# The state space layer's scaled C matrices: their transfers issued by GpSimd in place of ScalarE

## The chip, the cores and the metric

The kernel runs on one core of a Trainium2 chip. The metric is the time of one execution on the device in microseconds (us), as the median of several runs. The work is fp32 throughout; large matrix products are made as three matmuls each, from operands that are split into a high and a low half.

## What is computed

One inference step of a two-layer decoder trunk over 576 tokens (512 of a prompt and 8 samples of 8). Layer 0 has gated delta rule heads and a spatial gating MLP, layer 1 causal pooling groups and a diagonal state space layer. Each layer is followed by a squared-ReLU channel mixer and an embedding gate. The part that the change touches belongs to the state space layer, cut to its core here:

```
lam_bar = exp((lam_re + i lam_im) * exp(log_dt))          # 32 groups, 64 states each
b_bar   = (lam_bar - 1) / lam * (b_re + i b_im)           # [32, 64, 16]
s_t     = lam_bar * s_(t-1) + b_bar u_t                   # 16 channels per group
y_t     = real((c_re + i c_im) s_t) + d_skip * u_t
```

The kernel doesn't step through the tokens one by one. It works in chunks of 8 tokens, and needs for that the matrices B and C scaled by the powers of `lam_bar`: `C * lam_bar^(i+1)` for i = 0 to 7 carries the state at a chunk's start to each of its 8 outputs. These scaled C matrices depend on weights alone. They are made early, in a preparation, and written to a scratch array in DRAM, from which layer 1 reads them later.

## The kernel before

**The channel mixer of layer 0** (`ffn`) runs in two halves. In each half, 16 products with `up` make 16 hidden tiles, and 8 products with `down` consume them. A product goes through pieces of four weight blocks (`KU`): the weights of a piece are loaded by SyncE into `wraw` (four buffers), ScalarE casts them to the high half `whi` (line 93), VectorE subtracts to get the low half `wlo` (line 94), and TensorE runs 24 matmuls with them (`mm3`, lines 121 to 123). `whi` and `wlo` have three buffers each. Of a hidden tile, ScalarE makes the high half `hidh` (line 200).

**The preparation** (`s5_pre`) is a generator. `ffn` calls it twice at each of its steps, so that its work on GpSimd, VectorE, TensorE and ScalarE is interleaved with the channel mixer. Its loop runs over four quarters of the 32 groups. In each quarter it loads `s5b` and `s5c` (one buffer each, lines 1339 and 1340, issued by ScalarE), and GpSimd makes eight scaled B matrices in `s5WB` and then eight scaled C matrices in `s5CL`, each from the one before by six operations on 128 x 64 elements (lines 1348 to 1356). Both tiles have one buffer. The four transfers of line 1376 write `s5CL` to the scratch array `dCL`, by real and imaginary part `s` and by group parity `g`; each takes 64 partitions with four runs of 512 B. GpSimd then copies `s5c` into `s5Cb` (line 1380), TensorE multiplies `s5WB` with `s5Cb` (`s5pk`, line 1384) and transposes `s5WB` (`s5pw`, line 1392), and ScalarE copies and writes these out (lines 1393 and 1394). After the loop, the products `s5K` are written to a scratch array (line 1397), read back in another arrangement (`s5st`, line 1406) and copied by GpSimd (line 1409).

**What sets the order.** A scheduler simulates the program and lays down, for each engine, one order of instructions. An engine's queue is in order: an instruction that waits for another engine, a DMA issue included, holds all that stand behind it on its engine. ScalarE's queue carries the casts of the channel mixer as well as the transfers of the preparation.

Of the kernel before, what the change touches and what calls it, by code (L numbers as in the profile page):

```python
# [521 lines left out]
def bc(ap, n, axis):  # L522

    sh = list(ap.shape)
    v = ap.unsqueeze(axis)
    sh.insert(axis, n)
    return v.to_broadcast(sh)
# [649 lines left out]
def s5_pre(N, pool, I, D):  # L1177

    nc = N.nc
    gp = nc.gpsimd  # L1180
    mm, tr = nc.tensor.matmul, nc.tensor.transpose

    def tl(name, shape=(128, 16), **k):
        return pool.tile(list(shape), F32, name=name, **k)
# [151 lines left out]
    for q in range(4):  # L1336
        ps4 = slice(4 * q, 4 * q + 4)
        b_, c_ = tl("s5b", (128, 2, 4, 16)), tl("s5c", (128, 2, 4, 16))
        nc.scalar.dma_start(b_, I["s5b"][:, :, ps4])
        nc.scalar.dma_start(c_, I["s5c"][:, :, ps4])  # L1340
        WB = tl("s5WB", (128, 2, 4, 16, 8))
        CL = tl("s5CL", (128, 2, 4, 16, 8))
        x, y = tl("s5x", (128, 4, 16)), tl("s5y", (128, 4, 16))
        b16 = lambda v: bc(v[:, ps4], 16, 2)

        def cmul(o, a, l, conj):

            gp.tensor_mul(x, a[0], b16(l[0]))  # L1348
            gp.tensor_mul(y, a[1], b16(l[1]))
            (gp.tensor_add if conj else gp.tensor_sub)(o[0], x, y)  # L1350
            gp.tensor_mul(x, a[0], b16(l[1]))  # L1351
            gp.tensor_mul(y, a[1], b16(l[0]))  # L1352
            if conj:
                gp.tensor_sub(o[1], y, x)
            else:
                gp.tensor_add(o[1], x, y)

        lbs = (lb[:, 0], lb[:, 1])
        w = lambda j: (WB[:, 0, :, :, j], WB[:, 1, :, :, j])
        cl = lambda i: (CL[:, 0, :, :, i], CL[:, 1, :, :, i])  # L1360
        cmul(w(7), (b_[:, 0], b_[:, 1]), (fr, fi), False)
        yield
        for j in range(6, -1, -1):
            cmul(w(j), w(j + 1), lbs, False)
            if j % 2:
                yield

        gp.tensor_scalar(c_[:, 1], c_[:, 1], -1.0, None, op0=MUL)
        cmul(cl(0), (c_[:, 0], c_[:, 1]), lbs, True)
        for i in range(1, 8):  # L1370
            cmul(cl(i), cl(i - 1), lbs, True)
            if i % 2:
                yield
        for s in range(2):
            for g in range(2):
                nc.scalar.dma_start(D["CL"][64 * s:64 * s + 64, 8 * q + g:8 * q + 8:2],
                                    CL[64 * g:64 * g + 64, s].rearrange("p a c i -> p a (c i)"))
            yield
        for g in range(2):
            gp.tensor_copy(Cb[64 * g:64 * g + 64, :, :, g], c_[64 * g:64 * g + 64])  # L1380
        pk = N.sm.tile([128, 512], F32, name="s5pk", tag="sm")
        for a in range(4):
            for s in range(2):
                mm(pk[:, 32 * a:32 * a + 32], WB[:, s, a].rearrange("p c j -> p (c j)"),
                   Cb[:, s, a].rearrange("p g c -> p (g c)"), start=s == 0, stop=s == 1)
        nc.vector.tensor_copy(Kt[:, 8 * q:8 * q + 8].rearrange("p g c -> p (g c)"), pk[:, 0:128])
        yield
        st = tl("s5st", (128, 4, 2, 128))
        for s in range(2):
            pw1 = N.sm.tile([128, 512], F32, name="s5pw1", tag="sm")  # L1390
            for a in range(4):
                tr(pw1[:, 128 * a:128 * a + 128], WB[:, s, a].rearrange("p c j -> p (c j)"), N.ident)
            nc.scalar.copy(st[:, :, s], pw1.rearrange("p (a n) -> p a n", a=4))
        nc.scalar.dma_start(D["W1"][:, ps4], st)
        yield
# [327 lines left out]
def trunk(tc, I, O):  # L1723
    with ExitStack() as ctx:
# [35 lines left out]
        with N.banks(3, 2):  # L1760
            xs = N.norm_end()
            with tc.tile_pool(name="s5pre", bufs=1, reuse_waits="tile") as pool:
                pre = s5_pre(N, pool, I, D)
                p = ffn(N, h, xs, I["up0"], I["down0"], lambda m: N.norm_tile(h[m], col("norm_pe0", m)), I["p0"],
                        lambda: (next(pre, None), next(pre, None)))
                for _ in pre:
                    pass
            xs = N.norm_end()
            N.norm_begin()
            pe(N, h, xs, I["gate0"], I["proj0"], p, lambda m: N.norm_tile(h[m], col("norm_mix1", m)), True)  # L1770
            xs = N.norm_end()
            layer1(N, h, xs, I, O, V, D, lambda m: N.norm_tile(h[m], col("norm_ffn1", m)))
            xs = N.norm_end()
# [47 lines left out]
```

## Time and profile before

| | us |
|---|---|
| median of three runs | 1532.36 |
| lowest and highest of the three | 1529.27 and 1537.02 |
| the profiled execution, its own time | 1534.25 |
| span of the profiled execution (first to last instruction) | 1532.4 |

The page gives for each engine its busy time, the share of the span and the number of instructions. PE is TensorE, ACT ScalarE, DVE VectorE, POOL GpSimd, SP SyncE; ACTq and SPq are the DMA issues of these engines, which don't count as busy. A row of a timeline gives the start and the length in us, the engine, the line, the operation with the tiles it writes and reads, how many instructions were merged, and in brackets how long the engine had been idle before and what released it. A row that is released by "issue" followed DMA issues on the same engine. A row of the waits gives the waiting group, what ended its idle time, the total, the count and the longest. A table by windows gives the busy time and count of each engine in each stretch and the granted clock of TensorE as a share of full speed. A row of a line's instructions gives the shortest, median and longest duration in ns.

### The profile page before, as it was taken

How to read it: one execution, taken by the hardware profiler on the slowest of the kernel's cores; microseconds unless marked ns; L12 is line 12 of the kernel's file. 1: busy time of each engine (PE TensorE's matmuls, PEld its weight loads, DVE VectorE, ACT ScalarE, POOL GpSimd, SP SyncE). 2: the span in 40 equal slices, each digit the busy share in tenths (PEclk: the TensorE clock that was granted, in tenths of full speed). 3: DMA queues.
4: the chain of work that ended last, by engine and by line, in shares of the span. 5: the costliest groups of instructions: out<-in, count | busy, mean ns of one | idle time of the engine just before them, and what ended most of it. 6: DMA issues, size and time to landing. Idle time of an engine off the chain costs nothing.

```text
span 1532.4 us, 27273 instructions
## 1 busy us (share of the span) xinstructions
PE 1454.0 (95%) x10687; PEld 1422.4 (93%) x10687; DVE 944.6 (62%) x1680; ACT 593.0 (39%) x1121; POOL 429.4 (28%) x689
## 2 busy tenths in 40 slices
PE   7999999989998899999999998899999999999996
PEld 6888999968898899999999997899899999999995
DVE  6666446398954222546334669468877777676655
ACT  5462273224222112223334452255554444444452
POOL 4644244232786580821010116103000000000212
PEclk9999999999999999999999999599999999999998
DMA  5131111333223233255222383433232232321222
GB/s 193 49 96 49 39 42 58 112 119 102 95 96 99 83 95 112 90 138 159 83 84 75 112 265 108 141 90 122 83 90 89 87 95 77 96 94 54 70 88 71
DMA packets 107281, 149.46 MB, mean 98 GB/s; under 512 B 30800, under 2 KB 46544, under 8 KB 107152
## 3 DMA queue, kind: packets, MB, share of 16 engines
q1 hardware_dynamic: 78960, 128.63, 26.9%
q10 hardware_dynamic: 27616, 16.99, 4.0%
q8 instruction: 84, 1.38, 0.4%
q0 software_dynamic: 576, 2.10, 0.4%
q14 instruction: 45, 0.37, 0.1%
HBM read 130.73 MB, written 16.43 MB: 96 GB/s over the span
## 4 chain that ended last, share of the span: by engine, by line
PE 73%; DVE 13%; POOL 7%; issue 3%; ACT 3%; DMA 1%; ACTq 1%; SPq 0%; DVEq 0%; POOLq 0%
PE down L123 9%; PE down L121 8%; PE down L122 8%; PE up L121 2%; PE gate L121 2%; PE gate L123 2%; PE up L123 2%; PE gate L122 2%; PE up L122 2%; PE pp L535 2%; DVE Y L721 1%; DVE wlo L94 1%; POOL s5x L1351 1%; POOL s5x L1348 1%; POOL s5y L1352 1%
## 5 line engine op out<-in xcount | busy, mean ns | idle before, releaser
L93 ACT CAST whi<-wraw 128x512 fp32r<-128x512 f32 (+2 forms) x352 | 211.7, 605 | 490.3 <-PE down L122 176.1
L94 DVE TENSOR_TENSOR wlo<-wraw,whi 128x512 fp32r<-128x512 f32 (+1 forms) x306 | 219.5, 719 | 194.5 <-ACT whi L93 187.7
L121 PE MATMUL down<-hidh,whi 128*128 128x288 f32 x1024 | 304.7, 298 | 7.6 <-ACT whi L93 4.3
L123 PE MATMUL down<-hidh,wlo 128*128 128x288 f32 x1024 | 305.6, 299 | 0.0
L122 PE MATMUL down<-hidl,whi 128*128 128x288 f32 x1024 | 302.8, 296 | 0.0
L226 POOL TENSOR_TENSOR acc<-acc,sq 128x576 f32<-128x576 f32 x45 | 68.8, 1529 | 694.2 <-ACT sq L225 675.8
L121 PEld LDWEIGHTS down<-hidh,whi 128*128 128x128 f32 x1024 | 194.4, 190 | 8.1 <-ACT whi L93 4.5
L122 PEld LDWEIGHTS down<-hidl,whi 128*128 128x128 f32 x1024 | 196.2, 192 | 0.0
L123 PEld LDWEIGHTS down<-hidh,wlo 128*128 128x128 f32 x1024 | 194.2, 190 | 0.0
L121 PE MATMUL up<-xh,whi 128*128 128x288 f32 x576 | 172.3, 299 | 8.1 <-ACT whi L93 7.8
L123 PE MATMUL up<-xh,wlo 128*128 128x288 f32 x576 | 171.8, 298 | 2.4 <-DVE wlo L94 2.4
L122 PE MATMUL up<-xl,whi 128*128 128x288 f32 x576 | 171.5, 298 | 0.7 <-DVE xl L213 0.7
L121 PEld LDWEIGHTS up<-xh,whi 128*128 128x128 f32 x576 | 109.1, 189 | 9.2 <-ACT whi L93 9.0
L123 PEld LDWEIGHTS up<-xh,wlo 128*128 128x128 f32 x576 | 109.6, 190 | 3.8 <-DVE wlo L94 3.6
L122 PEld LDWEIGHTS up<-xl,whi 128*128 128x128 f32 x576 | 109.3, 190 | 1.3 <-DVE xl L213 1.3
L94 POOL TENSOR_TENSOR wlo<-wraw,whi 128x512 fp32r<-128x512 f32 x46 | 60.9, 1325 | 105.3 <-ACT whi L93 94.7
L121 PE MATMUL gate<-xh,whi 128*128 128x288 f32 x256 | 75.6, 295 | 0.0
L123 PE MATMUL gate<-xh,wlo 128*128 128x288 f32 x256 | 75.6, 295 | 0.0
L122 PE MATMUL gate<-xl,whi 128*128 128x288 f32 x256 | 75.5, 295 | 0.0
L371 DVE TENSOR_TENSOR h<-h,down 128x576 f32<-128x576 f32 x64 | 48.0, 749 | 39.6 <-PE down L123 39.6
L121 PE MATMUL qkv<-xh,whi 128*128 128x288 f32 x192 | 60.3, 314 | 0.8 <-ACT whi L93 0.8
L122 PE MATMUL qkv<-xl,whi 128*128 128x288 f32 x192 | 59.3, 309 | 0.0
(638 smaller groups left out, 3769.7 us busy)
## 6 DMA issues: line engine op xcount, KB each, us to landing
wraw<-in_down SPq DMA_DIRECT2D x128, 256.0 KB, 2.7
wraw<-in_up SPq DMA_DIRECT2D x72, 256.0 KB, 2.6
qraw<-in_up SPq DMA_DIRECT2D x56, 256.0 KB, 2.9
wraw<-in_wA SPq DMA_DIRECT2D x48, 256.0 KB, 2.6
wraw<-in_wout SPq DMA_DIRECT2D x32, 256.0 KB, 2.6
wraw<-in_gate SPq DMA_DIRECT2D x32, 256.0 KB, 2.6
S<-in_S SPq DMA_DIRECT2D x8, 512.0 KB, 3.8
wraw<-in_wcd SPq DMA_DIRECT2D x16, 256.0 KB, 4.0
```

The source lines that it names most:

```text
L93: nc.scalar.copy(hi, raw)
L94: self.lo.tensor_sub(lo, raw, f(hi))
L121: mm(o, hi, xh[:, s], start=start, stop=False)
L122: mm(o, hi, xl[:, s], start=False, stop=False)
L123: self.pe_last = mm(o, lo, xh[:, s], start=False, stop=stop)
L226: nc.gpsimd.tensor_add(self.acc, self.acc, sq)
L371: nc.vector.tensor_add(c3(h[m]), c3(h[m]), ps)
L535: N.pe_last = nc.tensor.matmul(*a, **k)
L721: nc.vector.scalar_tensor_tensor(Y, E[:, i:i + 600], w(i), Y, op0=MUL, op1=ADD)
L1348: gp.tensor_mul(x, a[0], b16(l[0]))
L1351: gp.tensor_mul(x, a[0], b16(l[1]))
L1352: gp.tensor_mul(y, a[1], b16(l[0]))
```

## The change

The four issues of line 1376, in each of the four quarters, are moved from ScalarE's queue to GpSimd's:

```
-                nc.scalar.dma_start(D["CL"][64 * s:64 * s + 64, 8 * q + g:8 * q + 8:2],
+                gp.dma_start(D["CL"][64 * s:64 * s + 64, 8 * q + g:8 * q + 8:2],
                                     CL[64 * g:64 * g + 64, s].rearrange("p a c i -> p a (c i)"))
```

The scheduler then lays down another order. On GpSimd, at the end of the first quarter (products of `s5CL` end, those of the second quarter's `s5WB` begin with `s5b`), the order changes like this:

```order
 L1351 TENSOR_TENSOR s5x<-s5CL,s5lb 128x64
 L1352 TENSOR_TENSOR s5y<-s5CL,s5lb 128x64
-L1354 TENSOR_TENSOR s5CL<-s5y,s5x 128x64
+L1376 DMA dCL<-s5CL 64x4x128 x2
+L1354 TENSOR_TENSOR s5CL<-s5y,s5x 128x64
+L1376 DMA dCL<-s5CL 64x4x128 x2
 L1348 TENSOR_TENSOR s5x<-s5b,s5fr 128x64
 L1349 TENSOR_TENSOR s5y<-s5b,s5fi 128x64
```

Two issues now stand ahead of the last product of C and two behind it; the same happens in the other three quarters. On ScalarE, at the same place in the program, between the casts of the `up` products:

```order
 L93 CAST whi<-wraw 128x512 x2
 L200 CAST hidh<-fs 128x576
-L1376 DMA dCL<-s5CL 64x4x128 x4
 L93 CAST whi<-wraw 128x512 x2
 L200 CAST hidh<-fs 128x576
```

The four issues are gone from between the casts. On ScalarE one quarter later, around the load of `s5c` for the third quarter (which overwrites the `s5c` that the second quarter's first C products read):

```order
 L93 CAST whi<-wraw 128x512 x2
 L200 CAST hidh<-fs 128x576
-L93 CAST whi<-wraw 128x512
 L1340 DMA s5c<-in_s5c 128x2x64
-L93 CAST whi<-wraw 128x512
-L200 CAST hidh<-fs 128x576
-L93 CAST whi<-wraw 128x512 x3
-L1376 DMA dCL<-s5CL 64x4x128 x4
-L93 CAST whi<-wraw 128x512 x5
+L93 CAST whi<-wraw 128x512 x2
+L200 CAST hidh<-fs 128x576
+L93 CAST whi<-wraw 128x512 x8
```

The second quarter's batch is gone, and the load stands one `whi` cast further forward than before, ahead of two casts in place of behind one of them. The order of SyncE's queue is the same as before.

## Rows read from the trace of the kernel before

**Rows 1.** The page's busy times, TensorE: us, share of the span, instructions.

```profile
PE 1454.0 (95%) x10687; PEld 1422.4 (93%) x10687; DVE 944.6 (62%) x1680; ACT 593.0 (39%) x1121; POOL 429.4 (28%) x689
```

**Rows 2.** Waits of PE between 414 and 720 us.

```profile
PE up L121 <- ACT whi L93: 7.8, 2, 6.5
PE down L121 <- ACT whi L93: 4.3, 1, 4.3
```

**Rows 3.** Timeline of PE: the matmuls that followed idle time.

```profile
446.81 0.40 PE L123 MATMUL up<-xh,wlo 128*128 128x288 f32 x1 [0.52 <-DVE wlo L94]
...
466.11 0.61 PE L121 MATMUL up<-xh,whi 128*128 128x288 f32 x1 [6.49 <-ACT whi L93]
...
523.51 0.61 PE L121 MATMUL down<-hidh,whi 128*128 128x288 f32 x1 [4.31 <-ACT whi L93]
...
662.91 0.40 PE L121 MATMUL up<-xh,whi 128*128 128x288 f32 x1 [1.33 <-ACT whi L93]
```

**Rows 4.** Table by windows: a stretch before, and the stretches behind two stalls.

```profile
core 0: us, PE busy (x) PEld busy (x) DVE busy (x) ACT busy (x) POOL busy (x), PEclk, DMA share, GB/s
440.00:459.60 19.60, 18.95 (x139) 18.25 (x137) 9.16 (x12) 4.11 (x7) 17.41 (x45) 1.00 0.18 59
...
466.10:471.50 5.40, 5.39 (x23) 5.40 (x24) 3.31 (x5) 1.66 (x3) 0.00 (x0) 0.51 0.45 134
...
523.50:529.50 6.00, 5.99 (x25) 5.99 (x26) 1.89 (x3) 1.00 (x2) 0.00 (x0) 0.50 0.52 151
```

**Rows 5.** Timeline of ScalarE: issues of line 1376 and the casts behind them.

```profile
462.64 2.68 ACTq L1376 DMA_DIRECT2D dCL<-s5CL  x4
465.43 1.14 ACT L93 CAST whi<-wraw 128x512 fp32r<-128x512 f32 x2 [11.15 <-issue]
...
522.84 1.66 ACT L93 CAST whi<-wraw 128x512 fp32r<-128x512 f32 x3 [12.59 <-issue]
...
577.78 0.62 ACT L93 CAST whi<-wraw 128x512 fp32r<-128x512 f32 x1 [6.92 <-POOL s5CL L1354]
```

**Rows 6.** Timeline of ScalarE: casts on both sides of two loads of `s5c`.

```profile
435.98 0.62 ACT L93 CAST whi<-wraw 128x512 fp32r<-128x512 f32 x1 [2.58 <-PE up L122]
...
445.09 1.14 ACT L93 CAST whi<-wraw 128x512 fp32r<-128x512 f32 x2
...
496.91 0.62 ACT L93 CAST whi<-wraw 128x512 fp32r<-128x512 f32 x1 [0.23 <-PE up L122]
...
503.17 0.62 ACT L93 CAST whi<-wraw 128x512 fp32r<-128x512 f32 x1 [5.64 <-POOL s5CL L1354]
```

**Rows 7.** Timeline of GpSimd: ends of quarters and what it waits for.

```profile
462.97 0.32 POOL L1352 TENSOR_TENSOR s5y<-s5CL,s5lb 128x64 f32<-128x64 f32 x1
...
473.75 1.21 POOL L1380 COPY s5Cb<-s5c 64x128 f32<-64x128 f32 x2 [9.44 <-PE s5pk L1384]
478.06 0.76 POOL L1350 TENSOR_TENSOR s5WB<-s5x,s5y 128x64 f32<-128x64 f32 x1 [3.10 <-PE s5pw L1392]
...
534.58 0.63 POOL L1380 COPY s5Cb<-s5c 64x128 f32<-64x128 f32 x2 [12.84 <-PE s5pk L1384]
...
679.62 2.01 POOL L1409 COPY s5tp<-s5st 128x1024 f32<-128x1024 f32 x1 [19.04 <-DMA wraw<-in_up]
```

**Rows 8.** Durations (ns) and starts of issues and products; last, two GpSimd rows.

```profile
L1376 ACTq DMA_DIRECT2D dCL<-s5CL x16: 582/636/656, 462.6 to 661.5; - x16
...
L1350 POOL TENSOR_TENSOR s5CL<-s5x,s5y x32: 323/329/756, 442.9 to 659.1; 128x64 f32<-128x64 f32 x32
...
L1014 POOL DMA_DIRECT2D out_delta_s<-S x4: 594/594/762, 319.6 to 344.2; - x4
...
DMA to landing us min/median/max: 3.0/3.3/4.6
...
328.69 0.59 POOL L1014 DMA_DIRECT2D out_delta_s<-S  x1
329.30 1.28 POOL L94 TENSOR_TENSOR wlo<-wraw,whi 128x512 fp32r<-128x512 f32 x1
```

## The prediction

> **What bounds the kernel now.** I read the page's busy times first: TensorE (PE) is busy 95% of the span [rows 1], so a change elsewhere is worth what it takes out of PE's idle time and out of the stretches in which PE runs at a lower clock. The page's list of issues then gives the moved transfers their place: the scaled C matrices are written out in 16 transfers on ScalarE's queue, between 462.6 and 661.5 us [rows 8]. That is the first channel mixer, into which the preparation of the state space layer is interleaved. So the next view is PE's waits in that stretch: twice on the cast `whi` in front of an "up" piece, 7.8 us together, and once in front of a "down" piece, 4.3 us [rows 2]. Nothing else there keeps PE waiting for more than a few microseconds.
>
> PE's timeline gives the three places: idle 6.49 us before 466.11, 4.31 us before 523.51, 1.33 us before 662.91 [rows 3]. The reader should then look at what ScalarE did just before the first two. Its queue is in order. At 462.64 it begins to issue four C transfers and its next cast, at 465.43, comes after 11.15 us of idle; the cast at 522.84 comes after 12.59 us, again right behind such a batch [rows 5]. The batch itself takes only 2.68 us in that row. The rest of the hold is a wait: the issue stands in ScalarE's queue until GpSimd has finished the matrices (its last products of the first quarter run at 462.97 [rows 7]), and the weight casts stand behind it. The third batch held ScalarE 6.92 us, up to 577.78 [rows 5], and PE has no idle row there. So PE tolerates a hold of some 6 us and pays for what is beyond it. That fits the code: three `whi` buffers, pieces of 24 matmuls, and a matmul about every 0.136 us (18.95 us for 139 [rows 4]), which is 3.3 us a piece and two pieces ahead.
>
> Idle is not all that PE pays. After the first two stalls the granted clock is 0.51 for 5.4 us and 0.50 for 6.0 us, the lower of its two levels (1.2 GHz), while it is 1.00 in the stretch ahead [rows 4].
>
> **What it removes.** Each of the four quarters loses its batch on ScalarE. 16 issues of 0.636 us are 10.2 us of ScalarE [rows 8], but this engine is not the bound, so I count only what reached PE.
> - First quarter: 6.49 us idle, and 5.4 us at 0.51, where half the work is lost: 5.4 x 0.49 = 2.6 us. Together 9.1 us.
> - Second quarter: 4.31 us, and 6.0 x 0.50 = 3.0 us. Together 7.3 us.
> - Third quarter: nothing, the hold was covered by the two pieces ahead.
> - Fourth quarter: 1.3 us, with no row of a lower clock behind it.
>
> The sum is 17.7 us. The casts that were held are then released by PE itself, as they are elsewhere. I count on that because the order shows no wait on GpSimd left in front of them at these three places.
>
> **What it adds on GpSimd.** 16 issues, four for each quarter, two before and two after the last product of C. The trace has two neighbours for the price. GpSimd's own issues of another transfer took 0.594 us, once 0.762; ScalarE's issues of this very transfer 0.582 to 0.656 [rows 8]. The neighbour on the right engine moves 128 runs of 4 KB, these move 256 runs of 512 B, so if the time goes by the run it doubles to 1.19 us. I take 0.76 us, the largest row of the right engine, and keep 0.59 and 1.19 for the range. A quarter costs GpSimd 3.0 us (2.4 to 4.8).
>
> Who waits for that? Behind the issues stand the first products of the next quarter's B matrices, then `s5Cb`, then the rest of the chain for B, and then the first readers of the next `s5c`.
> - After the first quarter GpSimd idles until PE has used the old B: the `s5Cb` copy at 473.75 and the product at 478.06 both wait for PE [rows 7]. PE comes there 9.1 us earlier, so the product may start at 469.0. GpSimd's own chain allows it at 462.97 + 0.32 + 1.0 for three products of 0.33 [rows 8] + 0.6 to 1.2 for the two copies [rows 7] + 4 issues, which is 464.9 to 465.5 plus 3.0, at most 468.5. The issues fit into a wait that is there already; they decide from 0.9 us each.
> - After the second quarter the copy at 534.58 waits 12.84 us for PE [rows 7]. 7.3 us of that go with the stall of the second place and 5.5 us are left over, more than 3.0. After the third, the wait is longer still.
> - After the fourth, GpSimd's next instruction starts at 679.62 after 19.04 us of waiting for the reordering transfers [rows 7]. These come earlier by the same few microseconds; the issues fit many times.
>
> The landing of the transfers is waited for by nobody near: the next C products are written some 25 us later, and the matrices are read back in layer 1. The SyncE queue keeps its order.
>
> **The wait that takes their place.** The third order listing, of ScalarE one quarter later, shows it. The load of `s5c` for the third quarter waits for GpSimd's first C products of the second, and in the change one more `whi` cast stands behind it. In the trace of before that load held ScalarE until the cast at 503.17, while the cast before it ran at 496.91 [rows 6]. If GpSimd and PE both shift by 9.1 us, the cast now behind the load runs 503.17 - 496.91 = 6.3 us late. The nearest row: the same load one quarter earlier pushed a cast from 435.98 + 3.3 = 439.3 to 445.09 [rows 6], 5.8 us late, and PE idled 0.52 us at 446.81 [rows 3]. I take 0.9 us for 0.4 us more. Every microsecond that GpSimd is later than 469.0 adds one here.
>
> **Sum.** 17.7 - 0.9 = 16.8 us off a profiled span of 1532.4 us, 1515.6 us. The profiled execution's own time is 1534.25 us, 1.85 us above its span, and the median of the three runs is 1532.36 us. The change should come off all of them alike, so I forecast 1532.36 - 16.8, about 1515.5 us. With 1.19 us an issue GpSimd is at most 465.5 + 4.8 - 469.0 = 1.3 us late, and the time is 1516.8. With 0.59 us the time stays at 1515.5. Further out nothing in layer 1 hangs on these 17 us: from there on all engines follow PE and move with it.
>
> **Rivals.**
> 1. The issues on GpSimd are stretched by VectorE, and the stall moves to the load of `s5c`. In this stretch GpSimd's product of 0.329 us took up to 0.756 us [rows 8], so an instruction can be held by something, by at least 0.43 us. Against it: the four GpSimd issues of before took 0.594 to 0.762 us, with no held one among them. Worked from rows: if three holds of 0.43 us fall on an issue of 0.76, it takes 2.0 us, the chain is 465.5 + 8.0 - 469.0 = 4.5 us late, PE idles 0.9 + 4.5 = 5.4 us and drops its clock, as after 4.31 us, for another 3.0 us. The gain is 17.7 - 8.4 = 9.3 us: 1523 us.
> The Trainium skill ("SBUF — State Buffer", section "SBUF: two separate sides") has a rule that speaks against the change: GpSimd can't write the descriptors of its transfers while a VectorE instruction in a two-port mode holds the port that both share, and its example is a transfer of 3.1 us in place of 0.62. By that figure an estimate for four issues is 12.4 us, and the sum would be about 1527 us; no row here shows such an issue.
> 2. Slower than before: GpSimd stands still until each transfer has landed. GpSimd's transfers land after 3.0 to 4.6 us [rows 8]; with 0.76 us of issue that is up to 5.4 us, four times 21.4 us. The chain is then 465.5 + 21.4 - 469.0 = 17.9 us late, PE loses 0.9 + 17.9 + 3.0 = 21.8 us at the load, and after the second quarter GpSimd is 17.9 + 21.4 - 5.5 - 21.8 = 12.0 us behind PE, of which ScalarE's tolerance covers some 6: another 6 us, and 3.0 for the clock. 17.7 - 21.8 - 9.0 is 13 us slower: 1545 us. It turns slower than before at about 4 us an issue. Against it: after the issue at 328.69 GpSimd's next instruction begins at 329.30, 0.61 us later, long before any landing [rows 8].
> 3. The change does nothing that can be measured: the casts find another wait at the same two places. Candidates are their weights (`wraw`, loaded four pieces ahead by SyncE) and the weights' low halves on VectorE. Behind the stalls the held casts ran back to back [rows 5], which speaks for weights that were there. 1530 to 1534 us.
>
> **How the numbers follow.** My forecast with its bounds (1511 to 1519): 0.72. Rival 1: 0.13, most of it below 1524.7. Rival 3: 0.08. Rival 2: 0.07. Runs of before spread from 1529.27 to 1537.02 us, so a median can lie 3 us off. The range runs from 1509 to 1526, taking in most of rival 1; what it leaves out is 0.2. About 0.5%, 7.7 us, is what a measurement of this kernel can tell from no change. Faster by more than that: 0.82; within: 0.11; slower: 0.07.
>
> **What would show it.** In the changed profile PE should have no idle row above 2 us on `whi` between 455 and 670 us, and no window at the lower clock there. The four issues should stand on GpSimd as one run after C, each below 1.2 us. A remaining wait should be the load of `s5c` at some 493 us with PE idle below 2 us. I am wrong if GpSimd's issues take 2 us or more, if its `s5Cb` copy no longer waits for PE after the first quarter, or if PE's stalls stay with another releaser.

## The result and the profile after

The changed kernel takes 1515.01 us (median of 4 runs, 1509.66 to 1516.74), the kernel before 1531.68 us in the same comparison: a ratio of 0.9886 with a 95% interval of 0.9866 to 0.9906. The forecast was 1515.5 us and faster. The profiled execution is the shortest of the four; what that means comes below.

The page of the changed kernel, busy times (answers to [rows 1]):

```profile
PE 1440.0 (95%) x10687; PEld 1409.9 (94%) x10687; DVE 946.5 (63%) x1680; ACT 592.9 (39%) x1121; POOL 446.2 (30%) x705
```

The waits of PE from 414 to 720 us (answers to [rows 2]: group, what ended the idle time, total us, times, longest):

```profile
PE down L121 <- ACT whi L93: 1.5, 1, 1.5
PE up L123 <- DVE wlo L94: 0.5, 1, 0.5
PE up L121 <- ACT whi L93: 0.3, 1, 0.3
PE down L123 <- DVE wlo L94: 0.2, 1, 0.2
```

The waits on `whi` of 7.8 and 4.3 us are gone, and one of 1.5 us is new. GpSimd has 16 instructions more, the issues. The windows at the places of the two stalls of [rows 4] show a TensorE that is never idle and at full clock; the third window is the stretch behind the new wait:

```profile
460.00:484.00 24.00, 24.00 (x186) 24.00 (x186) 13.01 (x19) 7.25 (x12) 21.51 (x50) 1.00 0.44 123
500.00:530.00 30.00, 30.00 (x234) 30.00 (x233) 8.15 (x12) 6.71 (x11) 21.76 (x56) 1.00 0.40 123
...
493.60:500.00 6.40, 6.20 (x45) 5.97 (x46) 5.00 (x7) 2.18 (x4) 5.93 (x13) 1.00 0.38 104
```

GpSimd's timeline at the end of the first quarter of the preparation (answers to [rows 7]):

```profile
464.26 1.35 POOL L1376 DMA_DIRECT2D dCL<-s5CL  x2
465.62 0.34 POOL L1354 TENSOR_TENSOR s5CL<-s5y,s5x 128x64 f32<-128x64 f32 x1
466.25 1.27 POOL L1376 DMA_DIRECT2D dCL<-s5CL  x2 [0.29 <-POOL s5CL L1354]
467.53 0.71 POOL L1348 TENSOR_TENSOR s5x<-s5b,s5fr 128x64 f32<-128x64 f32 x1
...
468.45 0.63 POOL L1380 COPY s5Cb<-s5c 64x128 f32<-64x128 f32 x2
469.16 0.33 POOL L1350 TENSOR_TENSOR s5WB<-s5x,s5y 128x64 f32<-128x64 f32 x1
```

All 16 issues by their durations (answers to [rows 8]):

```profile
L1376 POOL DMA_DIRECT2D dCL<-s5CL x16: 631/646/709, 464.3 to 648.0; - x16
```

A quarter's issues cost GpSimd 1.35 + 1.27 + 0.29 = 2.9 us, at 0.646 us each. The copy to `s5Cb` at 468.45 and the product at 469.16 no longer wait for PE. ScalarE goes from cast to cast without a batch between, up to the load of `s5c` (its timeline, answers to [rows 6]):

```profile
482.51 0.62 ACT L93 CAST whi<-wraw 128x512 fp32r<-128x512 f32 x1 [2.58 <-PE up L122]
...
492.25 0.55 ACTq L1340 DMA_DIRECT2D s5c<-in_s5c  x1
492.92 1.14 ACT L93 CAST whi<-wraw 128x512 fp32r<-128x512 f32 x2 [7.39 <-POOL s5CL L1354]
```

Behind it is the new idle row in PE's timeline (answers to [rows 3]):

```profile
493.59 0.40 PE L121 MATMUL down<-hidh,whi 128*128 128x288 f32 x1 [1.46 <-ACT whi L93]
```

**Where the time went.** Two profiles of this kernel can't be compared by their spans: runs differ by some microseconds in stages that the change doesn't touch. I therefore cut the profile at PE's own marks: the first `up` matmul, the last group of transposes (`s5pw`) of a quarter, and the first `gate` matmul, which comes after the channel mixer. Of before, two lines' instructions (shortest, median and longest in ns, first and last start), and PE's timeline at three marks:

```profile
L121 PE MATMUL up<-xh,whi x576: 288/295/610, 377.0 to 1082.8; 128*128 128x288 f32 x192
L121 PE MATMUL gate<-xh,whi x256: 288/295/297, 824.0 to 1511.3; 128*128 128x288 f32 x128
```

```profile
477.31 0.60 PE L1392 MATMUL s5pw<-ident,s5WB 128*128 128x128 f32 x4
537.34 0.60 PE L1392 MATMUL s5pw<-ident,s5WB 128*128 128x128 f32 x4
657.12 0.60 PE L1392 MATMUL s5pw<-ident,s5WB 128*128 128x128 f32 x4
```

And of after, the same two views:

```profile
L121 PE MATMUL up<-xh,whi x576: 288/295/442, 374.8 to 1059.2; 128*128 128x288 f32 x192
L121 PE MATMUL gate<-xh,whi x256: 288/295/297, 804.3 to 1486.6; 128*128 128x288 f32 x128
```

```profile
465.58 0.60 PE L1392 MATMUL s5pw<-ident,s5WB 128*128 128x128 f32 x4
521.07 0.60 PE L1392 MATMUL s5pw<-ident,s5WB 128*128 128x128 f32 x4
641.13 0.60 PE L1392 MATMUL s5pw<-ident,s5WB 128*128 128x128 f32 x4
```

From the first `up` to the first `gate` matmul it is 824.0 - 377.0 = 447.0 us before and 804.3 - 374.8 = 429.5 us after: 17.5 us less. Up to the first `up` this run was 2.2 us earlier, where nothing is changed. From the first to the last `gate` matmul it took 682.3 us against 687.3; the other kernels below, with the same work there, take 681.9 to 687.7. These 7 us are luck of this one profiled execution; the other three runs are 5 to 7 us longer than it. So I call the 17.5 us of this stretch the effect; the medians differ by 16.7.

The same marks for every kernel, in us; all differences below are read from this table:

| kernel | first `up` to 1st quarter's end | to 2nd's | to 4th's | to first `gate` | whole stretch |
|---|---|---|---|---|---|
| before | 100.3 | 60.0 | 119.8 | 166.9 | 447.0 |
| after | 90.8 | 55.5 | 120.1 | 163.2 | 429.5 |
| x1_after_again | 90.7 | 55.4 | 120.1 | 163.2 | 429.4 |
| x2_act_late | 90.6 | 53.3 | 120.1 | 163.2 | 427.1 |
| x3_s5c_four | 89.4 | 53.3 | 120.1 | 163.2 | 425.9 |
| x4_third_only | 101.2 | 58.8 | 119.8 | 167.0 | 446.8 |
| x5_first_only | 90.8 | 59.5 | 119.8 | 167.2 | 437.2 |
| x6_fourth_only | 100.5 | 60.2 | 120.1 | 163.1 | 443.9 |
| x7_hold_only | 96.7 | 54.7 | 124.8 | 166.8 | 443.0 |
| x8_late_c_four | 89.4 | 53.3 | 120.1 | 163.1 | 425.9 |
| x9_halves | 90.7 | 60.0 | 120.0 | 163.2 | 433.9 |
| x10_sync | 90.6 | 53.4 | 120.1 | 165.0 | 429.0 |

The effect is 9.5 us in the first quarter, 4.5 in the second, nothing in the third and 3.7 behind the fourth.

### The profile page after: what moved, and what is told of

It is laid out like the page before. It is cut to its first block, busy times and chain, and to the rows that moved or that the text cites. A ratio compares the mean times of both kernels' runs of the same rounds, so it can differ in the third digit from the quotient of the medians.

```text
span 1507.9 us, 27283 instructions
## 1 busy us (share of the span) xinstructions
PE 1440.0 (95%) x10687; PEld 1409.9 (94%) x10687; DVE 946.5 (63%) x1680; ACT 592.9 (39%) x1121; POOL 446.2 (30%) x705
## 4 chain that ended last, share of the span: by engine, by line
PE 76%; DVE 13%; POOL 5%; issue 3%; ACT 2%; DMA 0%; ACTq 0%; SPq 0%; DVEq 0%; POOLq 0%
PE down L123 9%; PE down L121 9%; PE down L122 9%; PE up L121 3%; PE up L122 3%; PE up L123 3%; PE gate L121 2%; PE gate L123 2%; PE gate L122 2%; PE pp L535 2%; DVE Y L721 1%; DVE wlo L94 1%; PE qx L189 1%; PE qy L190 1%; PE qz L191 1%
## 5 line engine op out<-in xcount | busy, mean ns | idle before, releaser
L94 DVE TENSOR_TENSOR wlo<-wraw,whi 128x512 fp32r<-128x512 f32 (+1 forms) x306 | 225.0, 736 | 177.0 <-ACT whi L93 174.2
```

The source lines that it names most:

```text
L94: self.lo.tensor_sub(lo, raw, f(hi))
```

## The experiments

The theory: an issue that waits holds ScalarE's queue, and the hold costs what TensorE then lacks. Its rivals: ScalarE's issue time was the cost; the gain was luck of a profile; the stalls would be found again elsewhere.

**x1_after_again**: the changed kernel, unedited.

> The changed kernel once more. The stretch that the change can touch is read on TensorE from the first matmul of an up projection to the first gate matmul of the next layer: 447.0 us in the profile before, 429.5 us in the profile of the changed kernel. The theory (an issue that waits holds the casts behind it on ScalarE) expects 428 to 431 us again, with one stall of 1 to 2 us left on TensorE near 493 us, at the load of s5c in the second quarter. If the 17.5 us were luck of one profile, the stretch would lie between the two. Total: 1510 to 1517 us.

Measured: 429.4 us, and 1515.59 us in all (ratio 0.9898, 0.9872 to 0.9924). This profile began its first `up` at 377.0, as before's did, and has the same idle row, of 1.40 us, at the load of `s5c`. The effect repeats to 0.1 us where the totals vary by 5.

**x2_act_late**: the transfers stay on ScalarE, at a place where GpSimd is done.

```
-            for g in range(2):
-                gp.dma_start(D["CL"][...], CL[...])
...
-        nc.scalar.dma_start(D["W1"][:, ps4], st)
+        w1 = nc.scalar.dma_start(D["W1"][:, ps4], st)
+        with N.tc.issue_after(w1.ins):
+            for s in range(2):
+                for g in range(2):
+                    nc.scalar.dma_start(D["CL"][...], CL[...])
```

> All sixteen transfers stay on ScalarE, but stand behind the write of W1 of the same quarter, where GpSimd has long made the tile, so that no issue waits for GpSimd. ScalarE pays the same sixteen issues of 0.67 us as before. Theory (the hold): the gain comes almost whole, 428 to 432 us from the first up matmul to the first gate matmul, 1511 to 1518 us in all, no ScalarE row waiting for s5CL ahead of a transfer; and the stall near 493 us is under 1 us, since GpSimd issues nothing there and its chain runs 2.9 us per quarter earlier. Rival (what ScalarE saves is the time of its issues): the stretch stays at 445 to 447 us and the total at 1529 to 1534 us.

Measured: 427.1 us, and 1510.40 us in all (0.9859, 0.9832 to 0.9886), both somewhat below the expected ranges. ScalarE's timeline:

```profile
468.12 0.33 ACTq L1391 DMA_DIRECT2D dW<-s5st  x1
468.49 2.74 ACTq L1395 DMA_DIRECT2D dCL<-s5CL  x4
471.27 0.62 ACT L93 CAST whi<-wraw 128x512 fp32r<-128x512 f32 x1 [2.67 <-PE up L123]
...
491.25 0.59 ACTq L1340 DMA_DIRECT2D s5c<-in_s5c  x1
491.96 1.14 ACT L93 CAST whi<-wraw 128x512 fp32r<-128x512 f32 x2 [5.20 <-POOL s5CL L1354]
```

The same four issues take the same 2.7 us of ScalarE, and the cast behind them is released by PE. All 17.5 us are there, and 2.4 more. So ScalarE's issue time cost nothing that shows here; the place of the issues in its order did. The load of `s5c` still holds ScalarE, 5.20 us instead of 7.39, and PE has no idle row behind it: the 2.2 us between the second quarters' ends of x2 and after (53.3 and 55.5) are the price of the new wait.

**x3_s5c_four**: after, with `tl("s5c", (128, 2, 4, 16), bufs=4)`.

> The changed kernel with four buffers for s5c in place of one: its four loads go out before the first quarter and never wait for GpSimd to be done with the quarter before. Theory (the stall left near 493 us is ScalarE held at the load of s5c by GpSimd's cmul chain): the cast after it no longer waits for the buffer of s5CL, the 1.5 us idle row of the down projection and the further 0.2 to 0.5 us beside it go, and the stretch from the first up matmul to the first gate matmul is 427 to 428.5 us, 1 to 2 us shorter than the changed kernel's. Rival (another wait stands close behind it, s5b's load or a WB buffer): the stretch stays at 429 to 430.5 us.

Measured: 425.9 us, better than expected, and 1508.91 us in all (0.9853, 0.9824 to 0.9881). PE has no idle row at all from 414 to 720 us. The 3.6 us to after are 2.2 in the second quarter, as in x2, and 1.4 in the first: the load of `s5c` for the second quarter, one quarter earlier, caused the waits of 0.3 us on `whi` and 0.5 us on `wlo` of the list above, which the expectation had left out.

**x4_third_only**: `(gp if q == 2 else nc.scalar).dma_start(...)`.

> Only the third quarter's four transfers go out from GpSimd; those of the first, second and fourth stay on ScalarE. In the profile before, the third quarter's hold of 6.92 us on ScalarE stood beside no idle row of TensorE. Theory (a hold costs only what TensorE then lacks): no gain, 446 to 448 us from the first up matmul to the first gate matmul, with the two large idle rows of 6.5 and 4.3 us in place. Rival (every quarter taken off ScalarE gives about a quarter of the gain): 442 to 443.5 us.

Measured: 446.8 us, and 1531.07 us in one run. Taking the third hold away gives nothing, and the idle rows of 6.5 and 4.3 us stand.

**x5_first_only**: the same with `q == 0`.

> Only the first quarter's four transfers go out from GpSimd. Theory: of the first quarter's hold all is got back (9.1 us), and of the others nothing: 437.5 to 440 us from the first up matmul to the first gate matmul, against 447.0 before and 429.5 in the changed kernel; the idle row of 4.3 us in the second quarter stays, and the new one of 1 to 2 us at the load of s5c (near 493 us) comes already here, since TensorE is some 9 us earlier there and GpSimd some 2.9 us later. Rival (the four parts do not add up: TensorE that is early at the first place waits as much longer at the second): 444 us or more.

Measured: 437.2 us, just under the expected range, and 1520.87 us in one run. The first quarter is 90.8 us, as in after. In the second, which is nearly as long as before, the cause has changed:

```profile
491.98 0.40 PE L121 MATMUL down<-hidh,whi 128*128 128x288 f32 x1 [1.46 <-ACT whi L93]
...
511.83 0.40 PE L121 MATMUL down<-hidh,whi 128*128 128x288 f32 x1 [1.71 <-ACT whi L93]
```

The idle row of 4.3 us, expected to stay, is 1.7 us, and the one at the load of `s5c` stands ahead of it, with a granted clock of 0.66 behind it (492 to 497 us). The parts don't add up place by place, though their total came out.

**x6_fourth_only**: the same with `q == 3`.

> Only the fourth quarter's four transfers go out from GpSimd. The profile before showed one idle row of 1.33 us there, and the prediction took 1.3 us; in the changed kernel TensorE made up some 3.5 us between the third quarter's and the fourth quarter's transposes. If the further 2.2 us belong to the fourth hold (refills and waits for wlo around that row), the stretch from the first up matmul to the first gate matmul is 443 to 444 us with the 6.5 and 4.3 us rows in place; if they belong to what the earlier quarters moved, it is 445.5 to 446 us.

Measured: 443.9 us, and 1524.10 us in one run (of which 5 us are luck behind the stretch: 681.9 us from first to last `gate`). The last part is 163.1 us, exactly after's. So the 3.7 us belong to the fourth hold alone (the whole stretch is 3.1 us shorter than before's, since its first three columns took 0.7 us more). Its price was 3.7 us, though the idle row says 1.3. The windows from 657 to 680 us, before and then x6:

```profile
657.00:680.00 23.00, 20.89 (x150) 19.72 (x149) 10.36 (x16) 7.19 (x12) 3.49 (x11) 1.00 0.57 141
```

```profile
657.00:680.00 23.00, 23.00 (x175) 23.00 (x174) 11.83 (x17) 7.24 (x12) 8.31 (x14) 1.00 0.70 192
```

25 matmuls are missing at full clock; at 23.0 / 175 = 0.131 us each that is 3.3 us, where the busy time shows 2.1 us of idle. The starts around the row tell why (before):

```profile
661.29 0.29 PE L123 MATMUL up<-xh,wlo 128*128 128x288 f32 x1
662.91 0.40 PE L121 MATMUL up<-xh,whi 128*128 128x288 f32 x1 [1.33 <-ACT whi L93]
663.15 0.29 PE L122 MATMUL up<-xl,whi 128*128 128x288 f32 x1
```

From start to start it is 1.62 us instead of 0.13: 1.49 are lost, the row says 1.33, and the next start comes after 0.24, another 0.1 late. A matmul's row is 0.29 us long, twice the rate, so each gap hides some 0.16 us before it counts as idle. Behind the hold come four more such small gaps, three with rows of 0.20, 0.20 and 0.27 us on `wlo`, and one without a row.

**x7_hold_only**: after, plus ScalarE copies that wait as the issues did.

```
                 gp.dma_start(D["CL"][...], CL[...])
+            nc.scalar.copy(tl("s5hold", (128, 1)), CL[:, s, 3, 15, 7:8])
             yield
```

> The changed kernel, with the transfers on GpSimd, and the hold put back alone: at the old place of the transfers ScalarE makes two copies of one column of s5CL per quarter (results not used), so that it waits for GpSimd's last products there and issues nothing. Theory (the wait in ScalarE's order is what cost the time, not the transfers): 442 to 449 us from the first up matmul to the first gate matmul, with idle rows of some 5 to 7 and 4 to 5 us on TensorE in the first and the second quarter and its clock at half behind them. Rival (the issues on ScalarE or the transfers' traffic cost the time): 429 to 432 us. The copies themselves cost ScalarE some 0.2 us each.

Measured: 443.0 us, and 1530.39 us in one run. ScalarE's timeline at the first quarter:

```profile
463.03 0.19 ACT L1378 COPY s5hold<-s5CL 128x1 f32<-128x1 f32 x1 [8.33 <-POOL s5CL L1350]
463.12 0.61 ACT L93 CAST whi<-wraw 128x512 fp32r<-128x512 f32 x1
465.35 0.19 ACT L1378 COPY s5hold<-s5CL 128x1 f32<-128x1 f32 x1 [1.61 <-POOL s5CL L1354]
```

PE's timeline, three idle rows:

```profile
463.79 0.40 PE L121 MATMUL up<-xh,whi 128*128 128x288 f32 x1 [3.79 <-ACT whi L93]
...
517.05 0.40 PE L121 MATMUL down<-hidh,whi 128*128 128x288 f32 x1 [0.45 <-ACT whi L93]
...
653.48 1.11 PE L1393 MATMUL s5pw<-ident,s5WB 128*128 128x128 f32 x4 [3.96 <-DVE s5K L1387]
```

A wait without any transfer costs 443.0 - 429.5 = 13.5 of the 17.5 us. The total was in the expected range, the places weren't: the scheduler put a cast between the two copies, so the first hold is shorter (3.79 us idle), the second nearly nothing, and the fourth dearer, where VectorE's copy `s5K` stood behind a `wlo` that waited for a held cast. By the table, 5.9 of the 13.5 us lie in the first quarter and 3.6 behind the fourth, where before pays too; 4.7 lie in the third column, most of them at `s5K`, where before pays nothing; and the second quarter is 0.8 us shorter than after's.

**x9_halves**: each transfer of GpSimd cut in two (`for k in range(2)`, half of the runs each).

> The changed kernel with each of GpSimd's transfers cut in two: 8 issues per quarter of 128 runs each in place of 4 of 256. If an issue on GpSimd is paid by the issue (0.65 us whatever it carries), GpSimd's chain gets 2.6 us per quarter longer, and the stall at the load of s5c near 493 us grows with it: from 55.5 us to 58 us between the last transposes of the first and the second quarter, 432 to 434 us from the first up matmul to the first gate matmul. If it is paid by the run (256 runs at 2.5 ns each), the eight issues take 0.3 to 0.4 us each and nothing grows: 429 to 430 us.

Measured: 433.9 us, and 1519.40 us in one run. GpSimd's timeline, the first quarter's eight issues:

```profile
466.94 2.50 POOL L1377 DMA_DIRECT2D dCL<-s5CL  x4
...
470.10 2.41 POOL L1377 DMA_DIRECT2D dCL<-s5CL  x4 [0.29 <-POOL s5CL L1354]
```

PE's timeline at the load of `s5c`, and the window behind it:

```profile
498.34 0.61 PE L121 MATMUL down<-hidh,whi 128*128 128x288 f32 x1 [3.54 <-ACT whi L93]
```

```profile
500.00:504.00 4.00, 4.00 (x18) 4.00 (x18) 2.57 (x4) 1.20 (x2) 3.61 (x8) 0.50 0.44 131
```

Half the runs cost nearly as much: 0.61 us by the median, against 0.65. So these issues of GpSimd are paid by the issue. 2.3 us more on GpSimd (2.50 + 2.41 for 1.35 + 1.27) are 4.5 us on PE: its idle row grows by 2.1, and the rest is a clock of 0.50 behind it, which after's shorter row didn't have. The second quarter is 60.0 us, where 58 were expected.

**x10_sync**: `nc.sync.dma_start(...)` for the same transfers.

> The sixteen transfers from SyncE, which issues the loads of the weight tiles (wraw, four buffers) and nothing else there. Theory (an issue that waits holds what stands behind it on its engine, and what that costs is what TensorE then lacks): in the first quarter the issues stand before a load that the changed kernel issues at about 451 to 454 us, and GpSimd is done at 463.5 to 466 us, so the loads behind them are 10 to 12 us late, with about 8 to 10 us of weight tiles in the buffers: a stall of 2 to 6 us on TensorE near 465 to 470 us, little or nothing in the other quarters, and no stall at the load of s5c, since GpSimd issues nothing: 428 to 434 us from the first up matmul to the first gate matmul. Rival (four buffers of weights cover the whole hold): 427 us, like the kernel with the transfers behind the W1 write.

Measured: 429.0 us, and 1515.92 us in one run (before on the same chip: 1528.74, one run). SyncE's timeline:

```profile
450.52 1.78 SPq L83 DMA_DIRECT2D wraw<-in_up  x2
464.85 2.76 SPq L1376 DMA_DIRECT2D dCL<-s5CL  x4
467.70 5.71 SPq L83 DMA_DIRECT2D wraw<-in_up  x5
```

SyncE issues nothing from 452.3 to 464.85, and yet the first quarter is 90.6 us: PE has no idle row there, so the four weight buffers cover the hold. The expected stall of 2 to 6 us there did not come, and the rival was right for this place. The second quarter is x2's, as expected; behind the fourth 1.8 us are lost, of which idle rows of 0.40, 0.20 and 0.19 us show 0.8. A hold goes where the queue leads, and costs by the depth of what that queue fills.

**x8_late_c_four**: x2 and x3 together.

> Both that helped, in one kernel: the sixteen transfers on ScalarE behind the write of W1 (GpSimd issues nothing), and four buffers for s5c (no load of it waits). Each by itself left the stretch from the first up matmul to the first gate matmul at 427.1 and 425.9 us. Theory: TensorE had no idle row left in the stretch with four buffers, so nothing is to be had beyond it: 425.5 to 426.5 us, and a total within 2 us of the kernel with four buffers alone, 1505 to 1512 us. Rival (the two gains add): 423.5 to 424.5 us.

Measured: 425.9 us, and 1509.83 us in all (0.9847, 0.9821 to 0.9873), the same as x3. PE isn't idle from 414 to 800 us in it; nothing more is to be had there. x3 and x8, about 1509 us, are the fastest versions; by the stretch they beat the change by 3.6 us.

## Why the prediction was right, point by point

- **The hold.** Right. x2 (issues, no hold) keeps the gain, x7 (hold, no issues on ScalarE) loses 13.5 us of it, 9.5 of them in the first quarter and behind the fourth.
- **First quarter, 9.1 us.** Measured 9.5. Idle row and half clock behind it, as summed.
- **Second quarter, 7.3 us, less a new wait of 0.9.** Alone it is 60.0 - 53.3 = 6.7 us, and the new wait costs 2.2. The place was right (`s5c`'s load issued at 492.25, forecast some 493), the size was not, and the failed step is "the product may start at 469.0": that the issues fit into a wait of GpSimd for PE which is there already. That wait is gone, which the prediction had named as a sign of being wrong ("if its `s5Cb` copy no longer waits for PE after the first quarter"). The product starts 469.16 - 374.8 = 94.4 us behind the first `up` matmul, not 469.0 - 377.0 = 92.0; by the prediction's own rule, a microsecond for a microsecond, these 2.4 us would make the new wait 3.3 us, and it measures 2.2. The term that failed in GpSimd's chain is 462.97, taken over from before as if GpSimd kept its pace. PE's last transposes come 9.5 us earlier in the stretch, and GpSimd's last C product of the first quarter, counted from the first `up` matmul, 4.4 us later: 463.37 - 377.0 = 86.4 us before, 465.62 - 374.8 = 90.8 after. The two issues ahead of it are 1.35 us. The other 3.0 have nothing to do with GpSimd's transfers: the same product is at 89.4 us in x2 and x10, which have none. It is GpSimd's arithmetic that got slower, once ScalarE's casts kept coming and VectorE worked on behind them. The 23 us from 63 us after the first `up`, before and after:

```profile
440.00:463.00 23.00, 18.96 (x139) 18.25 (x137) 9.16 (x12) 4.11 (x7) 20.33 (x55) 1.00 0.16 50
```

```profile
437.80:460.80 23.00, 22.14 (x165) 21.67 (x164) 12.75 (x17) 6.63 (x12) 20.65 (x48) 1.00 0.26 82
```

VectorE is busy 12.75 us instead of 9.16, and GpSimd, as busy as before, gets 48 instructions done instead of 55. Sixteen of its products for C take over 0.6 us, against nine before. Each of them starts while VectorE runs `wlo`, `hidl` or `fs` and ends 0.18 to 0.21 us behind that instruction (after, VectorE's timeline and GpSimd's):

```profile
455.08 0.68 DVE L94 TENSOR_TENSOR wlo<-wraw,whi 128x512 fp32r<-128x512 f32 x1
```

```profile
455.21 0.74 POOL L1354 TENSOR_TENSOR s5CL<-s5y,s5x 128x64 f32<-128x64 f32 x1
```

It depends on which instruction VectorE runs. In this kernel all operands of `wlo`, `hidl` and `fs` lie in SBUF, the memory of the tiles; `fa` and the sum into `h` read one operand from PSUM, the memory of TensorE's results. Beside `fa` a product keeps its length (after, the same two timelines):

```profile
454.41 0.76 DVE L285 TENSOR_TENSOR fa<-up,r 128x576 f32<-128x576 f32 x1 [0.60 <-PE up L123]
```

```profile
454.49 0.34 POOL L1351 TENSOR_TENSOR s5x<-s5CL,s5lb 128x64 f32<-128x64 f32 x1
```

Of the 384 products of the whole preparation in after, 93 start beside one of the first three and take 0.56 to 0.88 us. Of the 38 that start beside `fa` or `h`, all but one take 0.29 to 0.37 us (that one ends behind a `wlo` that began 0.02 us after it), and the other 253 take at most 0.35.

Seven more of the long rows at 0.42 us each are the 3.0 us. So rival 1 was wrong on what VectorE stretches (no issue: 0.631 to 0.709 us for all sixteen) and right that the stall at `s5c` grows by it. In the other kernels that product is at 86.3 to 87.7 us where ScalarE is held there, and at 89.4 to 91.9 where it isn't; but no run changed VectorE's work alone, so this cause is read from the traces and not isolated.
- **The Trainium skill's rule** ("SBUF — State Buffer", section "SBUF: two separate sides"), by which the sum would have been about 1527 us, wasn't put to the test. It asks for a VectorE instruction in a two-port mode, and the Trainium skill says in the same section, under "Who interferes with whom", that `tensor_tensor` has no such mode, but with both inputs in SBUF contends with GpSimd's reads. The trace agrees with the latter: the stretched products are those beside such instructions. In after, ten of the 16 issues have VectorE instructions beside them, `wlo`, `hidl` and `fa`, which are `tensor_tensor`, and once `fs`, a `scalar_tensor_tensor`; no issue is held by them. `hidl` runs from 464.18 to 464.94, beside the first issue, which takes 0.71 us; the issue at 511.87, with nothing of VectorE beside it, takes 0.69.
- **Third quarter, nothing.** Right: x4, 446.8 against 447.0.
- **Fourth quarter, 1.3 us.** Measured 3.7. The failed term is a price read from one idle row, where 25 matmuls were missing (x6).
- **The price of an issue, 0.76 us.** 0.646, and not by the run (x9), so the condition of the upper bound of 1.19 falls.
- **The sum.** 9.1 + 7.3 + 1.3 - 0.9 = 16.8 was forecast, 9.5 + 6.7 - 2.2 + 3.7 = 17.7 is measured (the stretch gives 17.5, with 0.3 lost in the third and fourth quarters). The two larger misses, 1.3 us too little for the new wait and 2.4 too little for the fourth quarter, have opposite signs, and the forecast is as close as it is partly by that.
- **Rivals 2 and 3** fall: GpSimd goes on 0.01 us after an issue (467.53), long before any landing (2.5 us at the least), and no other wait took the places of the two large ones.

## What to carry to other kernels

A DMA issue that waits for a slow producer belongs behind the point where that producer is done, or on a queue that has slack, and not ahead of work that feeds the busiest engine; moving it later on the same engine was as good here as moving it to the producer. Price a stall by matmul starts that are missing in a table by windows, not by the idle row alone. When a held engine is freed, ask which engines behind it now work more, and whom they slow down.

## What the runs showed of the hardware

- An issue of this transfer costs much the same on all three engines: 0.636 us on ScalarE, 0.646 on GpSimd, 0.610 on SyncE (medians), and 0.607 on GpSimd for half the runs.
- Small products on GpSimd (0.33 us) take some 0.75 us where they start beside a VectorE instruction with all operands in SBUF, and keep 0.33 us beside one that reads PSUM; issues on GpSimd aren't stretched beside either. In x2, whose GpSimd issues nothing there, the same chain of products took 3.0 us longer over 20 us.
- The granted clock behind a short stall differs from run to run: PE's idle row of 1.46 us is followed by 1.00 in after (493.6 to 500 us), and by 0.66 from 492 to 497 us in x5, a mix of its two levels, behind an idle row of the same 1.46 us. A fall didn't always cost, either. Behind the fourth hold the clock is 0.50 from 660.85 to 664.26 us in x4 and 1.00 from 657 to 680 us in before, with idle rows of 1.35 and 1.33 us, and the last part takes 167.0 and 166.9 us.
